# SwiGLU gate/up in seven-product block sums: a fourth such K pair per column block, and two pairs' low parts made by ACT and an adding DMA

## Chip, core and metric

One NeuronCore of a Trainium2 chip runs the whole program; the metric is device time in microseconds. TensorE (PE) multiplies, VectorE (DVE) and ScalarE (ACT) work on vectors, GpSimd (POOL) does little, SyncE (SP) issues the weight loads.

## What is computed

A two-layer encoder trunk on a 256 x 2048 input in float32. Layer 0 mixes by differential attention and a gated MLP, layer 1 by a gated linear recurrence; each layer ends with a SwiGLU FFN of hidden width 5632, and the FFN's first half is what the change touches.

```python
def swiglu(h, w_gate, w_up, w_down):
    return (jax.nn.silu(h @ w_gate) * (h @ w_up)) @ w_down

for l in range(DEPTH):
    h = h + mixer_l(rms_norm(h, mix_norm[l]))
    hn = rms_norm(h, ffn_norm[l])
    h = h + swiglu(hn, ffn_w_gate[l], ffn_w_up[l], ffn_w_down[l])
return rms_norm(h, final_norm)
```

## The kernel before

Weights come from HBM as float32 and are multiplied in three products each: the weight is split into a high part `whi` (ACT rounds the loaded tile `raw` to float32r) and a low part `wlo` (DVE subtracts, raw - whi), the activations likewise into `xh` and `xl`, and PE adds xh*whi, xh*wlo and xl*whi into one bank. `product` (L295 to L300) issues these three matmuls of 128 x 512; L297 and L299 read the high part of the weights, L298 the low part.

**FFN blocks.** The FFN (L394) walks 11 blocks of 512 hidden columns per layer, in the groups 0-1, 2-4, 5-7, 8-10; after each group the down projection of that group runs (`stream`, L128). Block j multiplies all of K = 2048 in eight pairs of 128-row chunks; `gate_up` (L289) handles them one after the other. For pair p one load of 1 MB brings four tiles of 128 x 512: gate and up columns of both chunks. `raw` and `whi` have three buffers, `wlo` two, shared with `stream`. Everything of the split runs ahead of its use by the priority `AHEAD`, and the scheduler writes out one fixed order per engine; each engine works through its order without overtaking.

**Two kinds of pairs.** Write a pair's K chunks and token halves as 2 x 2 blocks. An N pair takes eight products (24 matmuls) into the banks P2, P4, P5, P3. An S pair takes seven products (21 matmuls) into seven banks, with sums of weight tiles in place of some of the tiles: DVE forms four sums (L316 to L318), ACT rounds them to `thi` (L319), DVE makes `tlo` (L322). `thi`, `tlo` and the sums' tile `t` have one buffer each. The sums of activations (`make_combos`, L366) are formed once per layer during block 0, which uses eight N pairs. The string `PAIRS` gives the pattern of the other ten blocks: three S, five N.

**End of a block.** After the last S pair the banks P1, P6 and P7 are combined into `u` (L430 to L432); after the last pair DVE and ACT add up the other banks, apply silu and write `hh` (L444 to L448, L406, L407, L410), which PE transposes (L206) for the down projection.

Of the kernel before, what the change touches and what calls it, by code (L numbers as in the profile page):

```python
# [11 lines left out]
F32 = mybir.dt.float32  # L12
F32R = mybir.dt.float32r
# [3 lines left out]
ALU = mybir.AluOpType  # L17
# [28 lines left out]
WLO_BUFS = 2  # L46
# [26 lines left out]
def trunk(ctx: ExitStack, tc: tile.TileContext, ins, out):  # L73
    nc = tc.nc
# [20 lines left out]
    def bank(tag, shape, name):  # L95
        return psum[tag].tile(shape, F32, tag=tag, name=name)
# [18 lines left out]
    def tick():  # L115
        while pieces:
            try:
                next(pieces[0])
                return
            except StopIteration:  # L120
                pieces.pop(0)
# [162 lines left out]


    P1, P2, P3, P4, P5, P6, P7 = range(7)
    PAIRS = "NSNSNSNN"

    def gate_up(l, j, xs, combos, fx, name, plain, after):  # L289
        pattern = "N" * 8 if plain else PAIRS  # L290
        bk = [bank("mm", [P, NB], f"{name}_ps{i}") for i in range(4 if plain else 7)]
        uses = {"S": [P1, P2, P3, P6, P7, P4, P5], "N": [0, 1, 2, 3] if plain else [P2, P4, P5, P3]}
        seen, final = set(), {b: p for p in range(8) for b in uses[pattern[p]]}

        def product(b, p, x, w, end):  # L295
            (xh, xl), (hi, lo) = x, w
            nc.tensor.matmul(bk[b], xh, hi, start=b not in seen, stop=False)  # L297
            nc.tensor.matmul(bk[b], xh, lo, start=False, stop=False)  # L298
            nc.tensor.matmul(bk[b], xl, hi, start=False, stop=end and final[b] == p)  # L299
            seen.add(b)  # L300

        for p in range(8):
            raw = wpool.tile([P, 4, NB], F32, tag="raw", name=f"{name}_raw{p}")
            whi = wpool.tile([P, 4, NB], F32R, tag="whi", name=f"{name}_whi{p}")
            wlo = wpool.tile([P, 4, NB], F32R, tag="wlo", name=f"{name}_wlo{p}", bufs=WLO_BUFS)
            nc.sync.dma_start(raw, ins["w_gu"][l][j, p])
            fast = pattern[p] == "S"
            with tc.high_priority(offset=AHEAD):
                d = slice(0, 3 if fast else 4)
                nc.scalar.copy(whi[:, d], raw[:, d])  # L310
                if fast:

                    t = fx.tile([P, 4, NB], F32, tag="t", name=f"{name}_t{p}")
                    thi = fx.tile([P, 4, NB], F32R, tag="thi", name=f"{name}_thi{p}")
                    tlo = fx.tile([P, 4, NB], F32R, tag="tlo", name=f"{name}_tlo{p}")
                    nc.vector.tensor_tensor(t[:, 0:2], raw[:, 0:3:2], raw[:, 3:4].broadcast_to([P, 2, NB]), op=ALU.add)  # L316
                    nc.vector.tensor_tensor(t[:, 2], t[:, 0], raw[:, 2], op=ALU.add)
                    nc.vector.tensor_tensor(t[:, 3], t[:, 2], raw[:, 1], op=ALU.add)  # L318
                    nc.scalar.copy(thi, t)  # L319
                nc.vector.tensor_tensor(wlo[:, d], raw[:, d], whi[:, d].bitcast(F32), op=ALU.subtract)  # L320
                if fast:
                    nc.vector.tensor_tensor(tlo, t, thi.bitcast(F32), op=ALU.subtract)  # L322
            xs.get(min(p + 1, 7))
            xh, xl = xs.get(p)
            k0 = p % 2 * 2

            def x(c, b):
                s = slice(b * P, (b + 1) * P)
                return xh[:, k0 + c, s], xl[:, k0 + c, s]

            def w(i):
                return whi[:, i], wlo[:, i]

            if plain:
                for b, c, i in ((0, 0, 0), (0, 1, 1), (1, 0, 0), (1, 1, 1), (2, 0, 3), (2, 1, 2), (3, 0, 3), (3, 1, 2)):
                    product(b, p, x(c, b % 2), w(i), c == 1)
                    if (b, c) == (1, 1):
                        tick()
            elif fast:
                def sums(i):  # L340
                    return combos[p][0][:, i], combos[p][1][:, i]

                def tw(i):
                    return thi[:, i], tlo[:, i]

                product(P1, p, x(0, 0), w(0), True)
                product(P2, p, x(1, 0), w(1), True)
                product(P3, p, sums(2), w(2), True)
                product(P6, p, sums(1), tw(2), True)
                product(P7, p, sums(3), tw(1), True)  # L350
                product(P4, p, x(1, 1), tw(3), True)
                product(P5, p, sums(0), tw(0), True)
            else:
                for c in range(2):
                    product(P2, p, x(c, 0), w(c), c == 1)
                for c in range(2):
                    product(P4, p, x(c, 1), w(c), c == 1)
                for c in range(2):
                    product(P5, p, x(c, 1), w(3 - c), c == 1)
                for c in range(2):  # L360
                    product(P3, p, (combos[p][0][:, c], combos[p][1][:, c]), w(3 - c), c == 1)
            after(p, bk)
            tick()
        return bk

    def make_combos(xs, cp, combos, name):  # L366

        for p in range(8):
            xh, xl = xs.get(p)
            xt = _ap(xh, 0, [[KG * S, 2], [S, KG], [1, S]]).bitcast(F32)  # L370
            k0 = p % 2 * 2
            n = 4 if PAIRS[p] == "S" else 2
            c = [cp.tile([P, n, P], F32R, tag=f"c{p}{i}", name=f"{name}_c{p}{i}", bufs=1) for i in range(2)]
            parts = tmp.tile([P, 2, n, P], F32, tag="hh", name=f"{name}_cp{p}", bufs=2)

            def x(k, b):
                return xt[:, :, k0 + k, b * P:(b + 1) * P]

            if n == 4:

                nc.vector.tensor_tensor(parts[:, :, 0], x(0, 1), x(1, 1), op=ALU.subtract)
                nc.vector.tensor_tensor(parts[:, :, 1], parts[:, :, 0], x(0, 0), op=ALU.subtract)
                nc.vector.tensor_tensor(parts[:, :, 2], parts[:, :, 1], x(1, 0), op=ALU.add)
                nc.vector.tensor_tensor(parts[:, :, 3], x(0, 0), x(0, 1), op=ALU.subtract)
            else:
                for k in range(2):
                    nc.vector.tensor_tensor(parts[:, :, k], x(k, 0), x(k, 1), op=ALU.subtract)
            nc.vector.tensor_tensor(parts[:, 0], parts[:, 0], parts[:, 1], op=ALU.add)
            nc.scalar.copy(c[0], parts[:, 0])
            nc.vector.tensor_tensor(c[1], parts[:, 0], c[0].bitcast(F32), op=ALU.subtract)  # L390
            combos.append(c)
            yield

    def ffn(l, xs, rstd, following):  # L394

        with tc.tile_pool(name=f"hT{l}", bufs=3, reuse_waits="tile") as hp:
            scope = ExitStack()
            fx = scope.enter_context(tc.tile_pool(name=f"fx{l}", bufs=1, reuse_waits="tile"))
# [13 lines left out]
            for blocks in (range(0, 2), range(2, 5), range(5, 8), range(8, 11)):  # L412
                halves = Lazy()
                for j in blocks:
                    n = f"f{l}_{j}"
                    plain = j == 0
# [7 lines left out]
                    def after(p, bk):  # L424
                        if p in (1, 3) and halves.makers:
                            halves.get(len(halves.makers) - (2 if p == 1 else 1))
                        if not plain and p == PAIRS.rindex("S"):
                            with tc.high_priority(offset=2 * AHEAD):
# [4 lines left out]
                                early["u"] = u1, u2, u3  # L433

                    bk = gate_up(l, j, xs, combos, fx, n, plain, after)
                    hh = tmp.tile([P, 2, NB], F32, tag="hh", name=f"{n}_hh", bufs=2)
                    with tc.high_priority(offset=2 * AHEAD):
                        if plain:
                            for b in range(2):
# [33 lines left out]
                name = f"f{l}d{blocks[0]}_"  # L473
# [165 lines left out]
    for b in range(2):  # L639
# [8 lines left out]
        for half in range(2):  # L648
            v = vb[half][:, b, :]
            f = slice(half * NB, (half + 1) * NB)  # L650
# [58 lines left out]
    op = odd.enter_context(tc.tile_pool(name="odd", bufs=2, reuse_waits="tile"))  # L709

    def proj_c(nb, name, **kw):
        return stream(ins["hgrn_w_in"], [nb], ALLK, Groups(xs), f"c_{name}", **kw)[0]
# [103 lines left out]
    for hg in range(4):  # L816
# [30 lines left out]
        for d in range(2):  # L847
            ps = proj_c(4 + 4 * d + hg, f"f{d}{hg}")
            t = op.tile([P, 2, NB], F32, tag=f"f{d}", name=f"f{d}_{hg}", bufs=1)
# [15 lines left out]

    for nb in range(4):
        ps = proj_c(16 + nb, f"g{nb}", after=at_end(early) if nb == 3 else None)
        gt = tmp.tile([P, 2, NB], F32, tag="hh", name=f"g{nb}t", bufs=2)
        gated(ps, gt, True)
        if nb == 3:  # L870
            finish_pieces()
        nc.vector.tensor_tensor(o[nb], gt, o[nb], op=ALU.mult)
        xo.makers.append(lambda nb=nb: to_T(o[nb], xpool, "xT", f"co{nb}", gain_cols(SM_GN, nb)))
# [138 lines left out]
```

## Time and profile before

| | |
|---|---|
| median of 3 runs (lowest, highest) | 2433.96 us (2432.55, 2434.47) |
| the profiled execution | 2432.7 us, of which span 2430.9 us |
| PE, share of the span | 99% (11212 matmuls recorded) |
| DVE / ACT / POOL | 72% / 47% / 3% |
| granted PE clock, mean | 0.998 of full speed |
| loads | 442 MB on SP's queue, 52.1% of the 16 DMA engines |

An engine's busy share is over the whole span; a matmul's own duration (0.39 us here) overlaps that of the next, so PE's rate is read from start to start. In the names of the order rows below `f0_6_whi3` is layer 0, block 6, pair 3; `ps0` to `ps6` are the banks P1 to P7, and `x0_c20` is a sum of activations.

### The profile page before, as it was taken

What the parts mean: (1) busy time and instruction counts of PE and PEld (TensorE: products, weight loads), DVE (VectorE), ACT (ScalarE), POOL (GpSimd) and SP (SyncE); (2) the same over time, 40 slices, a digit from 0 to 9 for tenths busy, and PEclk for the clock granted to TensorE, in tenths of its full rate; (3) what the DMA queues carried; (4) which work ended last, traced back from release to release, by engine and by line L of the source; (5) the groups of instructions that cost most, each with busy time, mean ns of one, the idle gap of its engine ahead of it and who ended that gap; (6) DMA issues with size and microseconds to landing.
All of it is one profiled execution on the core that took longest, in us unless ns stands there. A gap on an engine that the chain in (4) does not pass through costs nothing.

```text
span 2430.9 us, 27555 instructions
## 1 busy us (share of the span) xinstructions
PE 2403.7 (99%) x11212; PEld 1993.8 (82%) x11212; DVE 1747.8 (72%) x1680; ACT 1136.2 (47%) x1048; POOL 72.9 (3%) x72
## 2 busy tenths in 40 slices
PE   8999999999999999999999999999999999999998
PEld 7887878888888888888888888888788888888887
DVE  5658667688678678754758595855777867876884
ACT  5445454445345445454444444444444544544553
POOL 0003000000000000000000000000000000000002
PEclk9999999999999999999999999999999999999999
DMA  7444455555555555555444444445455555565553
GB/s 275 169 160 168 160 180 184 190 194 204 191 202 196 191 198 190 201 198 191 156 145 151 156 139 156 144 168 190 169 195 200 187 201 191 190 208 190 208 208 139
DMA packets 63135, 445.50 MB, mean 183 GB/s; under 512 B 6944, under 2 KB 7200, under 8 KB 9760
## 3 DMA queue, kind: packets, MB, share of 16 engines
q1 hardware_dynamic: 62576, 442.13, 52.1%
q8 instruction: 88, 1.44, 0.2%
q10 hardware_dynamic: 432, 1.60, 0.2%
q14 instruction: 39, 0.32, 0.0%
HBM read 441.61 MB, written 2.10 MB: 183 GB/s over the span
## 4 chain that ended last, share of the span: by engine, by line
PE 94%; DVE 3%; POOL 1%; issue 1%; DMA 1%; ACT 0%; SPq 0%; ACTq 0%; POOLq 0%; DVEq 0%
PE f_ps L298 12%; PE f_ps L297 12%; PE f_ps L299 12%; PE f0d_ps L164 3%; PE f0d_ps L166 3%; PE f0d_ps L165 3%; PE f1d_ps L164 3%; PE f1d_ps L165 3%; PE f1d_ps L166 3%; PE c_f_ps L166 2%; PE c_f_ps L164 2%; PE c_f_ps L165 2%; PE s_l L759 2%; PE c_q_ps L166 1%; PE c_q_ps L164 1%; PE c_q_ps L165 1%
## 5 line engine op out<-in xcount | busy, mean ns | idle before, releaser
L310 ACT CAST f_whi<-f_raw 128x2048 fp32r<-128x2048 f32 (+1 forms) x176 | 311.2, 1768 | 248.7 <-PE f_ps L299 162.5
L320 DVE TENSOR_TENSOR f_wlo<-f_raw,f_whi 128x2048 fp32r<-128x2048 f32 (+1 forms) x176 | 368.7, 2106 | 47.0 <-PE f_ps L298 33.2
L297 PE MATMUL f_ps<-f_whi,f_x 128*128 128x512 f32 x848 | 331.3, 393 | 6.1 <-DVE h L883 3.1
L299 PE MATMUL f_ps<-f_whi,f_x 128*128 128x512 f32 x848 | 330.3, 390 | 0.0
L298 PE MATMUL f_ps<-f_wlo,f_x 128*128 128x512 f32 x848 | 330.1, 389 | 0.0
L297 PEld LDWEIGHTS f_ps<-f_whi,f_x 128*128 128x128 f32 x848 | 159.2, 188 | 38.8 <-ACT f_j L182 6.9
L299 PEld LDWEIGHTS f_ps<-f_whi,f_x 128*128 128x128 f32 x848 | 159.2, 188 | 33.6
L298 PEld LDWEIGHTS f_ps<-f_wlo,f_x 128*128 128x128 f32 x848 | 159.3, 188 | 32.2
L322 DVE TENSOR_TENSOR f_tlo<-f_t,f_thi 128x2048 fp32r<-128x2048 f32 x60 | 137.3, 2288 | 62.7 <-ACT f_thi L319 62.7
L319 ACT CAST f_thi<-f_t 128x2048 fp32r<-128x2048 f32 x60 | 114.8, 1913 | 132.3 <-DVE f_t L318 120.0
L149 ACT CAST f1d__whi<-f1d__raw 128x2048 fp32r<-128x2048 f32 x44 | 84.4, 1919 | 128.4 <-PE f1d_ps L166 97.6
L150 DVE TENSOR_TENSOR f1d__wlo<-f1d__raw,f1d__whi 128x2048 fp32r<-128x2048 f32 x44 | 100.8, 2290 | 60.6 <-PE f1d_ps L165 33.0
L150 DVE TENSOR_TENSOR f0d__wlo<-f0d__raw,f0d__whi 128x2048 fp32r<-128x2048 f32 x44 | 100.7, 2289 | 59.0 <-PE f0d_ps L165 29.3
L149 ACT CAST f0d__whi<-f0d__raw 128x2048 fp32r<-128x2048 f32 x44 | 84.4, 1918 | 122.1 <-PE f0d_ps L166 91.3
L150 DVE TENSOR_TENSOR c_f_wlo<-c_f_raw,c_f_whi 128x2048 fp32r<-128x2048 f32 x32 | 73.3, 2292 | 72.5 <-PE c_f_ps L165 60.5
L164 PE MATMUL c_f_ps<-c_f_whi,c_x 128*128 128x512 f32 x256 | 102.5, 400 | 0.0
L299 PE MATMUL f_ps<-f_whi,x_c 128*128 128x512 f32 x260 | 101.1, 389 | 0.0
L298 PE MATMUL f_ps<-f_wlo,x_c 128*128 128x512 f32 x260 | 101.1, 389 | 0.0
L297 PE MATMUL f_ps<-f_whi,x_c 128*128 128x512 f32 x260 | 101.1, 389 | 0.0
L166 PE MATMUL c_f_ps<-c_f_whi,c_x 128*128 128x512 f32 x256 | 100.2, 392 | 0.0
L165 PE MATMUL c_f_ps<-c_f_wlo,c_x 128*128 128x512 f32 x256 | 99.6, 389 | 0.0
L149 ACT CAST c_f_whi<-c_f_raw 128x2048 fp32r<-128x2048 f32 x32 | 61.2, 1913 | 77.6 <-PE c_f_ps L166 57.6
(536 smaller groups left out, 5637.1 us busy)
## 6 DMA issues: line engine op xcount, KB each, us to landing
f_raw<-in_w_gu SPq DMA_DIRECT2D x176, 1024.0 KB, 4.9
f0d__raw<-in_w_down SPq DMA_DIRECT2D x44, 1024.0 KB, 4.9
f1d__raw<-in_w_down SPq DMA_DIRECT2D x44, 1024.0 KB, 4.9
c_f_raw<-in_hgrn_w_in SPq DMA_DIRECT2D x32, 1024.0 KB, 4.9
eout_raw<-in_even_w_out SPq DMA_DIRECT2D x16, 1024.0 KB, 4.8
c_i_raw<-in_hgrn_w_in SPq DMA_DIRECT2D x16, 1024.0 KB, 4.8
c_q_raw<-in_hgrn_w_in SPq DMA_DIRECT2D x16, 1024.0 KB, 4.8
c_g_raw<-in_hgrn_w_in SPq DMA_DIRECT2D x16, 1024.0 KB, 4.9
```

Of the source, the lines that this page charges most:

```text
L149: nc.scalar.copy(whi[:, d], raw[:, d])
L150: nc.vector.tensor_tensor(wlo[:, d], raw[:, d], whi[:, d].bitcast(F32), op=ALU.subtract)
L164: nc.tensor.matmul(ps[b], xh[:, k, sl], hi[:, k, :], start=first, stop=False)
L165: nc.tensor.matmul(ps[b], xh[:, k, sl], lo[:, k, :], start=False, stop=False)
L166: nc.tensor.matmul(ps[b], xl[:, k, sl], hi[:, k, :], start=False, stop=end)
L297: nc.tensor.matmul(bk[b], xh, hi, start=b not in seen, stop=False)
L298: nc.tensor.matmul(bk[b], xh, lo, start=False, stop=False)
L299: nc.tensor.matmul(bk[b], xl, hi, start=False, stop=end and final[b] == p)
L310: nc.scalar.copy(whi[:, d], raw[:, d])
L319: nc.scalar.copy(thi, t)
L320: nc.vector.tensor_tensor(wlo[:, d], raw[:, d], whi[:, d].bitcast(F32), op=ALU.subtract)
L322: nc.vector.tensor_tensor(tlo, t, thi.bitcast(F32), op=ALU.subtract)
```

## The change

`PAIRS` becomes "SNSNSNSN": four S and four N pairs in the ten blocks that are not plain. An S pair's sums are written over `raw` itself (`t` is gone), after `wlo` has been made from it, so that `raw` is read until `tlo` is made. In all 11 blocks of a layer the low part of the N pairs 3 and 7 (`SUMMED`) is made in another way: ACT writes -whi into a tile `slo` (one buffer), and a DMA issued by POOL loads the same 1 MB of weights again and adds it to that tile. `hh` and the tiles that share its tag get one buffer instead of two. The order of three products in an S pair changes.

```diff
@@ -284,12 +284,14 @@
 
 
     P1, P2, P3, P4, P5, P6, P7 = range(7)
-    PAIRS = "NSNSNSNN"
+    PAIRS = "SNSNSNSN"
+
+    SUMMED = (3, 7)
 
     def gate_up(l, j, xs, combos, fx, name, plain, after):
         pattern = "N" * 8 if plain else PAIRS
         bk = [bank("mm", [P, NB], f"{name}_ps{i}") for i in range(4 if plain else 7)]
-        uses = {"S": [P1, P2, P3, P6, P7, P4, P5], "N": [0, 1, 2, 3] if plain else [P2, P4, P5, P3]}
+        uses = {"S": [P1, P2, P6, P7, P3, P4, P5], "N": [0, 1, 2, 3] if plain else [P2, P4, P5, P3]}
         seen, final = set(), {b: p for p in range(8) for b in uses[pattern[p]]}
 
         def product(b, p, x, w, end):
@@ -302,24 +304,30 @@
         for p in range(8):
             raw = wpool.tile([P, 4, NB], F32, tag="raw", name=f"{name}_raw{p}")
             whi = wpool.tile([P, 4, NB], F32R, tag="whi", name=f"{name}_whi{p}")
-            wlo = wpool.tile([P, 4, NB], F32R, tag="wlo", name=f"{name}_wlo{p}", bufs=WLO_BUFS)
+            if p in SUMMED:
+                wlo = fx.tile([P, 4, NB], F32R, tag="slo", name=f"{name}_slo{p}")
+            else:
+                wlo = wpool.tile([P, 4, NB], F32R, tag="wlo", name=f"{name}_wlo{p}", bufs=WLO_BUFS)
             nc.sync.dma_start(raw, ins["w_gu"][l][j, p])
             fast = pattern[p] == "S"
             with tc.high_priority(offset=AHEAD):
                 d = slice(0, 3 if fast else 4)
                 nc.scalar.copy(whi[:, d], raw[:, d])
                 if fast:
-
-                    t = fx.tile([P, 4, NB], F32, tag="t", name=f"{name}_t{p}")
+                    nc.vector.tensor_tensor(wlo[:, d], raw[:, d], whi[:, d].bitcast(F32), op=ALU.subtract)
+
                     thi = fx.tile([P, 4, NB], F32R, tag="thi", name=f"{name}_thi{p}")
                     tlo = fx.tile([P, 4, NB], F32R, tag="tlo", name=f"{name}_tlo{p}")
-                    nc.vector.tensor_tensor(t[:, 0:2], raw[:, 0:3:2], raw[:, 3:4].broadcast_to([P, 2, NB]), op=ALU.add)
-                    nc.vector.tensor_tensor(t[:, 2], t[:, 0], raw[:, 2], op=ALU.add)
-                    nc.vector.tensor_tensor(t[:, 3], t[:, 2], raw[:, 1], op=ALU.add)
-                    nc.scalar.copy(thi, t)
-                nc.vector.tensor_tensor(wlo[:, d], raw[:, d], whi[:, d].bitcast(F32), op=ALU.subtract)
-                if fast:
-                    nc.vector.tensor_tensor(tlo, t, thi.bitcast(F32), op=ALU.subtract)
+                    nc.vector.tensor_tensor(raw[:, 0:4:3], raw[:, 0:3:2], raw[:, 3:4].broadcast_to([P, 2, NB]), op=ALU.add)
+                    nc.vector.tensor_tensor(raw[:, 2], raw[:, 0], raw[:, 2], op=ALU.add)
+                    nc.vector.tensor_tensor(raw[:, 1], raw[:, 2], raw[:, 1], op=ALU.add)
+                    nc.scalar.copy(thi, raw)
+                    nc.vector.tensor_tensor(tlo, raw, thi.bitcast(F32), op=ALU.subtract)
+                elif p in SUMMED:
+                    nc.scalar.mul(wlo, whi.bitcast(F32), -1.0)
+                    nc.gpsimd.dma_start(wlo, ins["w_gu"][l][j, p], accum_op=ALU.add)
+                else:
+                    nc.vector.tensor_tensor(wlo, raw, whi.bitcast(F32), op=ALU.subtract)
             xs.get(min(p + 1, 7))
             xh, xl = xs.get(p)
             k0 = p % 2 * 2
@@ -345,10 +353,10 @@
 
                 product(P1, p, x(0, 0), w(0), True)
                 product(P2, p, x(1, 0), w(1), True)
+                product(P6, p, sums(1), tw(2), True)
+                product(P7, p, sums(3), tw(3), True)
                 product(P3, p, sums(2), w(2), True)
-                product(P6, p, sums(1), tw(2), True)
-                product(P7, p, sums(3), tw(1), True)
-                product(P4, p, x(1, 1), tw(3), True)
+                product(P4, p, x(1, 1), tw(1), True)
                 product(P5, p, sums(0), tw(0), True)
             else:
                 for c in range(2):
@@ -371,7 +379,7 @@
             k0 = p % 2 * 2
             n = 4 if PAIRS[p] == "S" else 2
             c = [cp.tile([P, n, P], F32R, tag=f"c{p}{i}", name=f"{name}_c{p}{i}", bufs=1) for i in range(2)]
-            parts = tmp.tile([P, 2, n, P], F32, tag="hh", name=f"{name}_cp{p}", bufs=2)
+            parts = tmp.tile([P, 2, n, P], F32, tag="hh", name=f"{name}_cp{p}", bufs=1)
 
             def x(k, b):
                 return xt[:, :, k0 + k, b * P:(b + 1) * P]
@@ -433,7 +441,7 @@
                                 early["u"] = u1, u2, u3
 
                     bk = gate_up(l, j, xs, combos, fx, n, plain, after)
-                    hh = tmp.tile([P, 2, NB], F32, tag="hh", name=f"{n}_hh", bufs=2)
+                    hh = tmp.tile([P, 2, NB], F32, tag="hh", name=f"{n}_hh", bufs=1)
                     with tc.high_priority(offset=2 * AHEAD):
                         if plain:
                             for b in range(2):
...
```

The same change of `bufs` stands once more in the gating of layer 1.

**What moves.** ACT's order around block 6 of layer 0, before, from the high part of pair 2 to that of pair 6:

```order
L310 CAST f0_6_whi2_5352<-f0_6_raw2_5351 128x2048
L406 ACTIVATE f0_5_s1_5264<-f0_5_g1_4986,f0_rstd_3003 128x512
L310 CAST f0_6_whi3_5382<-f0_6_raw3_5381 128x1536
L209 CAST f0_5T_x_5343<-f0_5T_tp0_5344 128x512
L310 CAST f0_6_whi4_5424<-f0_6_raw4_5423 128x2048
L319 CAST f0_6_thi3_5387<-f0_6_t3_5386 128x2048
L310 CAST f0_6_whi5_5454<-f0_6_raw5_5453 128x1536
L310 CAST f0_6_whi6_5495<-f0_6_raw6_5494 128x2048
```

and now, from the rounded sums of pair 0 to the negation of pair 7:

```order
L324 CAST f0_6_thi0_5303<-f0_6_raw0_5297 128x2048
L315 CAST f0_6_whi3_5404<-f0_6_raw3_5403 128x2048
L327 ACTIVATE f0_6_slo3_5405<-f0_6_whi3_5404 128x2048
L324 CAST f0_6_thi2_5375<-f0_6_raw2_5369 128x2048
L315 CAST f0_6_whi4_5442<-f0_6_raw4_5441 128x1536
L315 CAST f0_6_whi5_5476<-f0_6_raw5_5475 128x2048
L209 CAST f0_5T_x_5361<-f0_5T_tp1_5434 128x512
L315 CAST f0_6_whi6_5506<-f0_6_raw6_5505 128x1536
L324 CAST f0_6_thi4_5447<-f0_6_raw4_5441 128x2048
L315 CAST f0_6_whi7_5546<-f0_6_raw7_5545 128x2048
L327 ACTIVATE f0_6_slo7_5547<-f0_6_whi7_5546 128x2048
```

The negations (L327) stand right behind the high parts of pairs 3 and 7, and the rounded sums of pair 2 stand behind the first of them. (L209 rounds a transposed tile, as before.) DVE's order where block 5 ends and block 6 begins, before:

```order
L320 TENSOR_TENSOR f0_6_wlo0_5280<-f0_6_raw0_5278,f0_6_whi0_5279 128x2048
L444 TENSOR_TENSOR f0_5_g0_4985<-f0_5_ps1_4988,f0_5_u0_5189 128x512
L322 TENSOR_TENSOR f0_6_tlo1_5315<-f0_6_t1_5313,f0_6_thi1_5314 128x2048
L445 TENSOR_TENSOR f0_5_g1_4986<-f0_5_ps3_4990,f0_5_u2_5191 128x512
L446 TENSOR_TENSOR f0_5_hh_5255<-f0_5_ps4_4991,f0_5_u1_5190 128x512
L447 TENSOR_TENSOR f0_5_hh_5255<-f0_5_ps4_4991,f0_5_u2_5191 128x512
L448 TENSOR_TENSOR f0_5_hh_5255<-f0_5_ps2_4989,f0_5_hh_5255 128x512
L407 SCALAR_TENSOR_TENSOR f0_5_g0_4985<-f0_5_g0_4985,f0_rstd_3003,f0_5_s0_5261 128x512
L407 SCALAR_TENSOR_TENSOR f0_5_g1_4986<-f0_5_g1_4986,f0_rstd_3003,f0_5_s1_5264 128x512
L410 SCALAR_TENSOR_TENSOR f0_5_hh_5255<-f0_5_hh_5255,f0_rstd_3003,f0_5_g0_4985 128x512
L410 SCALAR_TENSOR_TENSOR f0_5_hh_5255<-f0_5_hh_5255,f0_rstd_3003,f0_5_g1_4986 128x512
L320 TENSOR_TENSOR f0_6_wlo1_5310<-f0_6_raw1_5308,f0_6_whi1_5309 128x1536
```

and now:

```order
L452 TENSOR_TENSOR f0_5_g0_5001<-f0_5_ps1_5004,f0_5_u0_5237 128x512
L322 TENSOR_TENSOR f0_6_raw0_5297<-f0_6_raw0_5297 128x512
L453 TENSOR_TENSOR f0_5_g1_5002<-f0_5_ps3_5006,f0_5_u2_5239 128x512
L415 SCALAR_TENSOR_TENSOR f0_5_g0_5001<-f0_5_g0_5001,f0_rstd_3006,f0_5_s0_5280 128x512
L454 TENSOR_TENSOR f0_5_hh_5274<-f0_5_ps4_5007,f0_5_u1_5238 128x512
L455 TENSOR_TENSOR f0_5_hh_5274<-f0_5_ps4_5007,f0_5_u2_5239 128x512
L456 TENSOR_TENSOR f0_5_hh_5274<-f0_5_ps2_5005,f0_5_hh_5274 128x512
L415 SCALAR_TENSOR_TENSOR f0_5_g1_5002<-f0_5_g1_5002,f0_rstd_3006,f0_5_s1_5283 128x512
L418 SCALAR_TENSOR_TENSOR f0_5_hh_5274<-f0_5_hh_5274,f0_rstd_3006,f0_5_g0_5001 128x512
L418 SCALAR_TENSOR_TENSOR f0_5_hh_5274<-f0_5_hh_5274,f0_rstd_3006,f0_5_g1_5002 128x512
L323 TENSOR_TENSOR f0_6_raw0_5297<-f0_6_raw0_5297 128x512
L330 TENSOR_TENSOR f0_6_wlo1_5333<-f0_6_raw1_5331,f0_6_whi1_5332 128x2048
```

Before, the sums of block 6's first S pair (pair 1, on `t`) stand ahead of these rows, and the low part of pair 1 comes right behind the ending. The sums of block 6's first pair now straddle the ending of block 5, and the low part of pair 1 is the second instruction behind it. PE's order at the same place, now:

```order
L301 MATMUL f0_5_ps2_5005<-f0_5_whi7_5244,x0_c71_3009 128x512
L299 MATMUL f0_6_ps0_5290<-f0_6_whi0_5298,f00_x_2612 128x512
L300 MATMUL f0_6_ps0_5290<-f0_6_wlo0_5299,f00_x_2612 128x512
L301 MATMUL f0_6_ps0_5290<-f0_6_whi0_5298,f00_x_2612 128x512
L299 MATMUL f0_6_ps1_5291<-f0_6_whi0_5298,f00_x_2612 128x512
L300 MATMUL f0_6_ps1_5291<-f0_6_wlo0_5299,f00_x_2612 128x512
L301 MATMUL f0_6_ps1_5291<-f0_6_whi0_5298,f00_x_2612 128x512
L299 MATMUL f0_6_ps1_5291<-f0_6_whi1_5332,f00_x_2612 128x512
L299 MATMUL f0_6_ps0_5290<-f0_6_whi2_5370,f01_x_2665 128x512
L206 MATMUL f0_5T_tp0_5362<-ident_89,f0_5_hh_5274 128x128 x4
L300 MATMUL f0_6_ps1_5291<-f0_6_wlo1_5333,f00_x_2612 128x512
```

Eight matmuls and four transposes stand between block 5's last product and the first that reads `wlo1`; before, 24 matmuls of pair 0 stood there ahead of pair 1. PE's first read of `slo3` is the 64th row from that read of `wlo1` on, its first read of `slo7` is 88 rows further, and `whi3` is read for the last time 22 rows after the first read of `slo3`. In the changed program's allocation raw1, raw3, raw5 and raw7 of a block share one of the three buffers of `raw`, raw0 and raw4 another, raw2 and raw6 the third: raw3's load waits until `wlo1` is made, raw4's until `tlo0` is.

## Rows read from the trace of the kernel before

**Rows 1.** The page: span, busy time, and the chain that ended last, by engine.
```profile
span 2430.9 us, 27555 instructions
...
PE 2403.7 (99%) x11212; PEld 1993.8 (82%) x11212; DVE 1747.8 (72%) x1680; ACT 1136.2 (47%) x1048; POOL 72.9 (3%) x72
...
PE 94%; DVE 3%; POOL 1%; issue 1%; DMA 1%; ACT 0%; SPq 0%; ACTq 0%; POOLq 0%; DVEq 0%
```

**Rows 2.** Engines by stretch, 546 to 549 us and most of layer 0's FFN.
```profile
core 0: us, PE busy (x) PEld busy (x) DVE busy (x) ACT busy (x) POOL busy (x), PEclk, DMA share, GB/s
546.00:549.00 3.00, 3.00 (x17) 2.51 (x16) 3.00 (x4) 2.25 (x2) 0.00 (x0) 1.00 0.98 382
645.00:1000.00 355.00, 355.00 (x1583) 292.87 (x1582) 276.27 (x222) 168.11 (x111) 0.00 (x0) 1.00 0.56 196
```

**Rows 3.** Who waited for whom: total us, times, longest us.
```profile
PE e_tp L206 <- DMA h<-in_x: 6.1, 1, 6.1
PE f_ps L297 <- DVE h L883: 3.1, 1, 3.1
...
ACT f_whi L310 <- PE f_ps L299: 162.5, 74, 6.0
ACT f_thi L319 <- DVE f_t L318: 120.0, 43, 6.2
```

**Rows 4.** The tile tlo: what PE's idle time before it ended with (us, times).
```profile
  DVE f_tlo L322: 4.9, 15
```

**Rows 5.** PE in order of time, 602.1 to 603.75 us: start, duration; eight matmuls.
```profile
602.14 0.39 PE L298 MATMUL f_ps<-f_wlo,f_x 128*128 128x512 f32 x1
...
603.73 0.39 PE L299 MATMUL f_ps<-f_whi,f_x 128*128 128x512 f32 x1
```

**Rows 6.** DVE's groups of instructions by form: busy us, mean ns.
```profile
L320 DVE TENSOR_TENSOR f_wlo<-f_raw,f_whi 128x2048 fp32r<-128x2048 f32 x116 | 264.8, 2289 | 47.0 <-PE f_ps L298 33.2 <-issue 11.2 <-PE f1d_ps L165 1.1
L322 DVE TENSOR_TENSOR f_tlo<-f_t,f_thi 128x2048 fp32r<-128x2048 f32 x60 | 137.3, 2288 | 62.7 <-ACT f_thi L319 62.7
L320 DVE TENSOR_TENSOR f_wlo<-f_raw,f_whi 128x1536 fp32r<-128x1536 f32 x60 | 105.1, 1752 | 0.0
...
L316 DVE TENSOR_TENSOR f_t<-f_raw 128x1024 f32<-128x1024 f32 x60 | 73.3, 1222 | 20.4 <-DMA f_raw<-in_w_gu 19.6 <-DVE f_wlo L320 0.3
...
L318 DVE TENSOR_TENSOR f_t<-f_t,f_raw 128x512 f32<-128x512 f32 x60 | 41.3, 689 | 1.1
```

**Rows 7.** ACT in order of time, 547 to 553 us: high parts and rounded sums.
```profile
547.33 1.91 ACT L310 CAST f_whi<-f_raw 128x2048 fp32r<-128x2048 f32 x1
549.16 1.91 ACT L319 CAST f_thi<-f_t 128x2048 fp32r<-128x2048 f32 x1
552.18 1.49 ACT L310 CAST f_whi<-f_raw 128x1536 fp32r<-128x1536 f32 x1 [1.11 <-PE f_ps L299]
```

**Rows 8.** DVE in order of time where block 2 ends and block 3 begins.
```profile
536.60 0.68 DVE L447 TENSOR_TENSOR f_hh<-f_ps,f_u 128x512 f32<-128x512 f32 x1
537.20 0.68 DVE L448 TENSOR_TENSOR f_hh<-f_ps,f_hh 128x512 f32<-128x512 f32 x1
537.80 1.53 DVE L407 SCALAR_TENSOR_TENSOR f_g<-f_g,f_rstd,f_s 128x512 f32<-128x512 f32 x2
539.25 1.41 DVE L410 SCALAR_TENSOR_TENSOR f_hh<-f_hh,f_rstd,f_g 128x512 f32<-128x512 f32 x2
540.57 1.75 DVE L320 TENSOR_TENSOR f_wlo<-f_raw,f_whi 128x1536 fp32r<-128x1536 f32 x1
```

**Rows 9.** The chain that ended last, at 546 us: four transposes.
```profile
546.17 0.44 PE f_2T_tp L206 x4
```

**Rows 10.** SP's queue: what its loads waited for: total us, times, longest us.
```profile
SPq L306 <- DVE f_wlo L320: 653.5, 128, 9.3
```

**Rows 11.** DMA issues: KB each, median us from issue to landing.
```profile
f_raw<-in_w_gu SPq DMA_DIRECT2D x176, 1024.0 KB, 4.9
```

**Rows 12.** PE in order of time at the start of the program, 7.7 to 10.1 us.
```profile
7.77 0.80 PE L164 MATMUL e_q_ps<-e_q_whi,e_x 128*128 128x512 f32 x1
8.89 0.80 PE L165 MATMUL e_q_ps<-e_q_wlo,e_x 128*128 128x512 f32 x1 [0.33 <-DVE e_q_wlo L150]
...
10.07 0.40 PE L165 MATMUL e_q_ps<-e_q_wlo,e_x 128*128 128x512 f32 x1
```

More of the change, by code (lines that the diff above doesn't have):

```diff
@@ L867, in trunk @@
         ps = proj_c(16 + nb, f"g{nb}", after=at_end(early) if nb == 3 else None)
-        gt = tmp.tile([P, 2, NB], F32, tag="hh", name=f"g{nb}t", bufs=2)
+        gt = tmp.tile([P, 2, NB], F32, tag="hh", name=f"g{nb}t", bufs=1)
         gated(ps, gt, True)
```

## Prediction

> **What bounds the kernel now.** I read the page first. The span is 2430.9 us, PE is busy for 2403.7 of it, and the chain that ended last runs over PE for 94% [rows 1]. The windows show the same inside layer 0's FFN: PE is busy for all of 355 us at granted clock 1.00, while DVE has 276.27 of them, ACT 168.11 and the loads a DMA share of 0.56 [rows 2]. So time is lost or won only where PE idles or issues fewer rows. The list of waits tells how near the other engines are: PE's largest waits are single ones of 6.1 and 3.1 us at the start and the end, whereas ACT waits 162.5 us for PE to free `whi` and 120.0 us for DVE's sums [rows 3]. The preparation is thus ahead of PE, but through few buffers. The one place of an S pair where PE idles is `tlo`: 15 waits, 4.9 us in all over 60 S pairs [rows 4]. The profiled execution took 2432.7 us, 1.3 less than the median of the runs; the sum is made against it and 1.3 is added at the end.
>
> **A. Fewer products.** Each of the 20 blocks that are not plain turns one N pair into an S pair, 24 matmuls into 21. In PE's order of time eight matmuls start within 1.59 us, seven steps, 0.227 us each [rows 5]. 60 x 0.227 = **-13.6 us**. For this DVE is hardly relieved. With the durations by form [rows 6], an N pair's low part costs 2.29 and an S pair 1.75 + 1.22 + 2 x 0.69 + 2.29 = 6.64: per block 5 x 2.29 + 3 x 6.64 = 31.4 before, 2 x 2.29 + 4 x 6.64 = 31.1 now. ACT gets 44 negations at 1.91 (nearest row: its cast of the same tile) and 20 more rounded sums at 1.91 [rows 7]; PE hides the durations themselves, since ACT has half its time free [rows 2], and what counts is their place, in C and D. The single buffer of `hh` costs nothing: its next writer comes a whole block later, and the sums of activations lie beside block 0's products; uncovered, one hand-over of 0.1 us a block. The order of three products in an S pair moves no work.
>
> **B. The boundary of two blocks.** The last product of a block releases DVE's ending. In the trace of before the last of the `hh` sums, the gating and the start of the next low part follow one another: 0.60 us for L448, 1.45 for two L407, 1.32 for two L410 [rows 8]. Now DVE has, from the last product to the end of `wlo1`, 0.60 + 0.72 (one L415) + 1.32 + 0.69 (the sum L323) + 2.29 = 5.62 us [rows 6, 8]. PE has eight matmuls, 1.82, and four transposes, 0.44 [rows 9], together 2.26, and then reads `wlo1`. Before, 24 matmuls (5.4) and the transposes covered the same ending. So PE idles 5.62 - 2.26 = 3.36 us where a block follows a block directly: blocks 3, 4, 6, 7, 9 and 10 of both layers, 12 times, **+40 us**. With starts (5.4) or full durations and a hand-over (5.9) it is 38 to 44.
>
> **C. S pairs that are fed later.** Sums now stand in `raw`, which is held until `tlo` is made; SP's loads already spend 653.5 us waiting for DVE to be done with a buffer [rows 10], so these loads start later. The rounded sums of pair 2 also stand behind a negation of 1.91 us on ACT. Low end: the 80 pairs wait as the 60 did, 4.9 x 20 / 60 = +2 [rows 4]. High end: the whole negation shows at `thi` in 20 blocks, +38. I take 0.33 us, the mean of the present waits, for three pairs of four, 60 x 0.33 = **+20 us**.
>
> **D. The adding load.** This is the largest term, and no row shows such a transfer. Let L be the time from the end of the negation to the landing of the sum. POOL is otherwise idle in the FFN and nothing but these loads stands in its order there, so its own wait for the negation delays nobody else.
> - Pair 3: raw3's load starts when `wlo1` is made. The load takes 4.9 [rows 11], the high part and the negation 1.91 each [rows 7], three hand-overs 0.3: 9.0. In that time PE goes from its first read of `wlo1` to `slo3`, 61 matmuls and some transposes: 61 x 0.227 + 0.44 + 0.4 of waits = 14.7. The slack is 5.7; PE stalls L - 5.7.
> - Pair 7: after `slo3` has landed PE reads it in 22 rows, 5.0; then ACT rounds `whi6` (1.49, held by the buffer of `whi3`), the sums of pair 4 (1.83 start to start), `whi7` (1.83) and negates (1.91) [rows 7], with hand-overs 12.4. PE has 88 rows, 20.0. The slack is 7.6; PE stalls L - 7.6.
>
> Together 2L - 13.3 in each of 22 blocks. Low end for L: the plain load of 1 MB, 4.9, which would stall nothing. High end: two such loads in series behind one raw load at the full rate of 382 GB/s [rows 2], 2 x 4.9 + 2.75 = 12.6. The transfer reads its destination, adds and writes, so the nearest row is the load, twice: **L = 10**. Then 6.7 x 22 = **+147 us**; with the ends 0 and +262 (11.9 x 22).
>
> The trace has no adding transfer to hold a rule against. The Trainium skill ("Collectives: The Full Stack", section "Why ReduceScatter is half of AllGather") says that an add in the DMA engine is dear not by the adding but by a second source read; by it and the row of 382 GB/s an estimate of L is 4.9 + 2.75 = 7.65, and the sum would come to +91 instead of +194. No run here shows it yet.
>
> **Sum.** -13.6 + 40 + 20 + 147 = +194; 2432.7 + 194 + 1.3 = **2628 us**. A difference under 0.2% (4.9 us) can't be told from none here.
>
> **The rivals.**
> 1. *The adding load costs one more pass of its bytes and no more*: L = 7.65 by the rate row [rows 2]. Stalls 1.95 + 0.05 a block, +44; total +91, **2525 us**. For it: the loads' engines are 44% free. Against it: SP's next loads run at the same time.
> 2. *The adding load is hidden*, L up to 5.7, because it is no dearer than a plain load. Then A + B + C remain: +47, **2481 us**. Against it: two reads and a write can hardly go as fast as one of each.
> 3. *The adding load is slow*, for example by many small pieces or by competing with raw loads: at L = 20 the stalls are 26.7 x 22 = 587, **3069 us**. It decides from L = 13 on.
> 4. *PE's clock falls in the gaps.* Gaps of about 4 us come some 40 times. In the trace the first two matmuls behind 6 us without work took 0.80 us and later ones 0.40 [rows 12], though the granted clock of that stretch reads 1.00; if all 22 products between a gap and the last read of `whi3` ran at half speed, 5 us each, it would be 40 x 5 = +200, **2828 us**. The Trainium skill ("TensorE: Matmul & The Clock Gate", Part 1) has the clock at 1.2 GHz after PE has been idle; before, the granted clock shows nothing of it, because PE hardly idles.
> 5. *Faster: PE stays the bound.* The mechanism is the three matmuls saved per block, with all preparation arriving in time; the place is each of the 20 blocks, the price -13.6, and it decides from stalls under 0.68 us a block. It needs L below 5.7 and a boundary where DVE gets through its ending in 2.3 us. For it: before, no ending shows as a wait of PE at all [rows 3]. Against it: 5.62 us of DVE's rows. **2420 us**. If the stalls just eat the saving, the time is the same.
>
> **How the numbers follow.** Chances: the forecast (L from 9 to 13) 0.40; rival 1 (L from 6 to 9) 0.20; rival 2 0.08; rival 3 0.17; rival 4 0.08; faster 0.05; the same 0.02. All but the last two are slower: 0.93. The range goes from just under rival 2 (2475) to rival 4 (2830, which also is L = 14.7); outside lie faster, same and most of rival 3, just under 0.2.
>
> **What would show it.** In the changed profile: matmuls fewer by 60; PE's waits on `slo` as the largest of all, some 4 us for pair 3 and 2 for pair 7, with L in the DMA list near 10; waits at `wlo1` of 3.4 us, 12 times, whose chain goes over DVE's L418 and L323; small waits at `thi` and `tlo`. B is wrong if PE waits at `wlo1` less than 2 us; D is wrong if the list shows a landing under 6 or over 13 us, or if `raw` loads slow beside it; the clock rival shows as a granted clock below 1.00 in the FFN.

## The result, and the profile after

The changed kernel takes 2660.99 us (median of 4 runs, 2655.96 to 2670.75), before 2434.22 us: ratio 1.0931, 95% interval 1.0906 to 1.0957, or 227 us slower. The prediction said 2628 us with a range of 2475 to 2830. The total is close; its make-up is not, as the profile shows. In the views below, PE is TensorE, PEld its weight loads, and a landing is the end of a transfer.

The page of the changed kernel: span, busy times, the sixteen DMA engines by queue (packets, MB, share of the span) and the chain by engine, against [rows 1].

```profile
span 2658.4 us, 27661 instructions
...
PE 2485.9 (94%) x11152; PEld 2025.5 (76%) x11152; DVE 1751.2 (66%) x1720; ACT 1245.8 (47%) x1112; POOL 110.6 (4%) x116
...
q1 hardware_dynamic: 62576, 442.13, 46.6%
q0 software_dynamic: 6336, 46.14, 8.8%
...
PE 69%; DMA 17%; ACT 6%; DVE 5%; issue 2%; POOL 1%; SPq 0%; ACTq 0%; POOLq 0%
```

PE issues 60 matmuls fewer and is yet busy 82.2 us longer, and it idles 2658.4 - 2485.9 = 172.5 us where it idled 27.2. Both matter. Transfers, 1% of the chain before, are 17% of it now. The idle part stands in the list of PE's waits (total us, times, longest us), against [rows 3]:

```profile
PE f_ps L300 <- DMA f_slo<-in_w_gu: 106.7, 36, 5.7
PE f_ps L300 <- DVE f_wlo L330: 27.1, 12, 2.3
PE e_tp L206 <- DMA h<-in_x: 6.0, 1, 6.0
PE f_ps L299 <- DVE h L891: 3.5, 1, 3.5
PE f_ps L299 <- DVE h L279: 3.3, 1, 3.3
PE f_ps L300 <- DVE f_tlo L325: 3.1, 8, 0.5
```

The adding loads and the twelve block boundaries make 134 us of it. Smaller waits show at the weight loads of the FFN's products, where before, apart from the start of each FFN, only `tlo` stood, first those of before:

```profile
PEld f_ps L298 <- DVE f_tlo L322: 4.8, 14, 0.6
```

and now:

```profile
PEld f_ps L299 <- ACT f_thi L324: 9.9, 19, 1.3
PEld f_ps L299 <- ACT f_whi L315: 8.6, 18, 0.6
PEld f_ps L300 <- DVE f_tlo L325: 7.8, 17, 0.8
```

That is 26.3 - 4.8 = 21.5 us more. What makes PE's busy time longer is seen behind one wait, in PE's order of time at 659 to 670 us:

```profile
659.68 0.39 PE L299 MATMUL f_ps<-f_whi,f_x 128*128 128x512 f32 x1
664.83 0.79 PE L300 MATMUL f_ps<-f_slo,f_x 128*128 128x512 f32 x1 [4.76 <-DMA f_slo<-in_w_gu]
665.42 0.63 PE L301 MATMUL f_ps<-f_whi,f_x 128*128 128x512 f32 x1
665.85 0.63 PE L299 MATMUL f_ps<-f_whi,f_x 128*128 128x512 f32 x1
...
670.07 0.40 PE L300 MATMUL f_ps<-f_slo,f_x 128*128 128x512 f32 x1
670.30 0.39 PE L301 MATMUL f_ps<-f_whi,f_x 128*128 128x512 f32 x1
```

and in the windows there (columns as in [rows 2]):

```profile
665.00:670.00 5.00, 5.00 (x12) 3.94 (x13) 1.12 (x3) 0.72 (x1) 0.00 (x0) 0.50 0.96 406
670.00:680.00 10.00, 10.00 (x47) 8.24 (x47) 7.50 (x9) 4.29 (x3) 0.00 (x0) 1.00 0.00 1
```

After 4.76 us of waiting the granted clock is 0.50, the 1.2 GHz level, and matmuls start 0.43 us apart, not 0.227: twelve in 5 us where 22 would fit. The wait thus costs 4.76 us and then some 2.5 more. The mean granted clock of the whole run fell from 0.998 to 0.968: 0.032 x 2658.4 - 0.002 x 2430.9 = 80 us of clock that PE did not get, some of it while waiting. Counted in starts, the matmuls within twenty rows behind the 48 waits on `slo` and at `wlo1` lost 63 us.

The account of the 227.5 us of span: idle +145.3 (the two large waits 134, the rest the boundary's transposes and small waits), busy +82.2. The latter is -13.6 for the matmuls saved, 60 to 80 for the clock and some 20 for the weight loads.

The adding loads' time from issue to landing (44 of them, min, median, max), and two pieces of the chain in block 9 of layer 0, first that of pair 3, then that of pair 7:

```profile
DMA to landing us min/median/max: 7.7/8.5/12.7
```

```profile
1026.11 8.24 DMA f_slo<-in_w_gu
...
1047.10 12.40 DMA f_slo<-in_w_gu
```

The median hides two cases. Over the 22 blocks pair 3's load lands after 8.3 us in the median and PE waits about 45 us for it in all; pair 7's lands after 11.8 us and PE waits 62 us. Around the second piece (the DMA view from 1040 to 1064 us) three raw loads for the next block share the engines:

```profile
q1 hardware_dynamic: 432, 3.15, 36.7%
q0 software_dynamic: 144, 1.05, 21.5%
...
f_raw<-in_w_gu SPq DMA_DIRECT2D x3, 1024.0 KB, 8.5
```

In 24 us the raw loads took 0.367 x 24 / 3 = 2.9 us each of all sixteen engines, the adding one 5.2, together 14.0. The raw loads begin to be issued at 1044.9 us and `slo7` lands at 1059.5, so the engines had work nearly all that time. Two of the raw loads land before the load that PE waits for, the third 1.3 us behind it. They are slowed as well: 8.5 us in the median, against 5.0 over the whole run.

### The profile page after: what moved, and what is told of

It reads as the page before. It is cut to its first block, busy times and chain, and to the rows that moved or that the text cites. A ratio compares the mean times of both kernels' runs of the same rounds, so it can differ in the third digit from the quotient of the medians.

```text
span 2658.4 us, 27661 instructions
## 1 busy us (share of the span) xinstructions
PE 2485.9 (94%) x11152; PEld 2025.5 (76%) x11152; DVE 1751.2 (66%) x1720; ACT 1245.8 (47%) x1112; POOL 110.6 (4%) x116
## 4 chain that ended last, share of the span: by engine, by line
PE 69%; DMA 17%; ACT 6%; DVE 5%; issue 2%; POOL 1%; SPq 0%; ACTq 0%; POOLq 0%
DMA f_slo<-in_w_gu 14%; PE f_ps L300 6%; PE f_ps L301 6%; PE f_ps L299 5%; PE f0d_ps L164 3%; PE f0d_ps L165 3%; PE f0d_ps L166 3%; PE f1d_ps L166 3%; PE f1d_ps L164 3%; PE f1d_ps L165 3%; DMA f_raw<-in_w_gu 3%; ACT f_whi L315 2%; ACT f_slo L327 2%; PE c_f_ps L166 2%; PE c_f_ps L164 2%; PE c_f_ps L165 2%
## 5 line engine op out<-in xcount | busy, mean ns | idle before, releaser
L299 PE MATMUL f_ps<-f_whi,f_x 128*128 128x512 f32 x768 | 321.3, 419 | 7.9 <-DVE h L891 3.5
L301 PE MATMUL f_ps<-f_whi,f_x 128*128 128x512 f32 x768 | 317.9, 417 | 0.0
L325 DVE TENSOR_TENSOR f_tlo<-f_raw,f_thi 128x2048 fp32r<-128x2048 f32 x80 | 183.3, 2291 | 129.2 <-ACT f_thi L324 129.2
L300 PE MATMUL f_ps<-f_slo,f_x 128*128 128x512 f32 x272 | 128.0, 471 | 106.8 <-DMA f_slo<-in_w_gu 106.7
L300 PE MATMUL f_ps<-f_wlo,f_x 128*128 128x512 f32 x496 | 199.6, 402 | 27.1 <-DVE f_wlo L330 27.1
L317 DVE TENSOR_TENSOR f_wlo<-f_raw,f_whi 128x1536 fp32r<-128x1536 f32 x80 | 140.5, 1756 | 103.6 <-PE f_ps L300 69.9
L324 ACT CAST f_thi<-f_raw 128x2048 fp32r<-128x2048 f32 x80 | 152.2, 1903 | 72.7 <-DVE f_raw L323 72.5
L300 PEld LDWEIGHTS f_ps<-f_slo,f_x 128*128 128x128 f32 x272 | 60.8, 224 | 137.3 <-DMA f_slo<-in_w_gu 124.4
L330 DVE TENSOR_TENSOR f_wlo<-f_raw,f_whi 128x2048 fp32r<-128x2048 f32 x52 | 119.0, 2288 | 23.3 <-ACT f_whi L315 20.1
L300 PEld LDWEIGHTS f_ps<-f_wlo,f_x 128*128 128x128 f32 x496 | 95.9, 193 | 49.5 <-DVE f_wlo L330 29.9
L300 PE MATMUL f_ps<-f_tlo,x_c 128*128 128x512 f32 x240 | 95.8, 399 | 3.3 <-DVE f_tlo L325 3.1
```

The source lines that it names most:

```text
L324: nc.scalar.copy(thi, raw)
L325: nc.vector.tensor_tensor(tlo, raw, thi.bitcast(F32), op=ALU.subtract)
```

## Experiments

All differences below are against the kernel before, run on the same chip.

**The S pairs without the adding loads.** The low parts of pairs 3 and 7 are DVE's again, in the two buffers of `wlo`.

```diff
-    SUMMED = (3, 7)
+    SUMMED = ()
```

> The changed kernel with the low parts of pairs 3 and 7 made by DVE again; the four S pairs and their sums over raw stay. Theory (the adding loads and the half clock behind their waits are most of the loss): the 107 us of waits on slo go, and nearly all matmuls at half rate with them; what is left is the boundary, 12 waits of 2.3 us and some 10 us of half clock behind them, less 13.6 for the saved matmuls: 2450 to 2480 us. Rival A (the four S pairs with sums over raw are the loss, because raw is held and loads start late): PE's waits move to wlo and tlo and the time stays over 2540 us.

Measured: 2528.5 us, ratio 1.0373 (1.0356 to 1.0391), +92 us, granted clock 0.980. The waits on `slo` are gone and 134 us with them, so the adding loads are the larger half. But the time lies 48 us above the theory's range for the rest, and 11 us under Rival A's; of the waits that Rival A named, `tlo` has only 18.4 us, at the weight loads. PE's waits (the transposes have six lines like the second, 23.1 us in all):

```profile
PE f_ps L300 <- DVE f_wlo L330: 26.2, 12, 2.3
...
PE f_2T_tp L206 <- DVE f_hh L418: 3.9, 4, 1.7
```

The boundary costs 49 us of waits here and puts the clock down: 146 matmuls of half rate, 0.2 us each, stand behind the twelve waits at `wlo1`, 29 us.

**The adding loads without the fourth S pair.** The pattern of before, pairs 2 and 6 by adding load.

```diff
-    PAIRS = "SNSNSNSN"
-
-    SUMMED = (3, 7)
+    PAIRS = "NSNSNSNN"
+
+    SUMMED = (2, 6)
```

> The other half of the change alone: three S pairs in the order of before (first pair an N pair), sums over raw, and the low parts of the N pairs 2 and 6 by negation and adding load. Theory: the boundary waits at wlo go, the waits on slo stay at 2 to 4.5 us each and put the clock to half speed behind them as in the changed kernel: granted clock about 0.97, 2530 to 2640 us. Rival A (the S pairs are the loss): under 2470 us, with few waits on slo.

Measured: 2576.83 us, ratio 1.0566 (1.0547 to 1.0586), +141 us, clock 0.979; 38 waits on `slo`, 85.7 us, the longest 4.3. No boundary wait of more than 0.2 us is left, as 24 matmuls of an N pair stand first again. This is as the theory had it.

**Sums over raw alone.** `PAIRS` as before, `SUMMED` empty; the sums' place, the single `hh` buffer and the order of three products in an S pair stay of the change.

> Before's three S pairs and all low parts on DVE, with only the sums written over raw and hh in one buffer. Theory: raw is held longer, but PE has enough lead: no wait over 1 us in the FFN, 2434 to 2446 us, granted clock 1.00. Rival A (holding raw is dear): the loads land late in each S pair, over 0.5 us in 60 pairs, above 2465 us.

Measured: 2454.90 us, ratio 1.0076 (1.0061 to 1.0091), +19 us. Neither number was right: the longest wait of PE inside the blocks is 2.05 us, the clock is at 0.996, but there are 50 small waits at the weight loads for `tlo` (15.7 us, before 4.8) and 12 for `whi` (9.1). That `raw` is held is seen in two more lists. ACT's waits for a raw load before it can round it, before and here, and the loads on SP's queue that wait here until `tlo` is made:

```profile
ACT f_whi L310 <- DMA f_raw<-in_w_gu: 12.3, 11, 1.9
```

```profile
ACT f_whi L315 <- DMA f_raw<-in_w_gu: 153.7, 58, 5.3
...
SPq L311 <- DVE f_tlo L325: 175.6, 52, 7.0
```

So writing the sums over `raw` has a price of its own. How much of the 19 us is due to it, and how much to the `hh` buffer and the order of products, this run does not separate.

**No adding.** The load into `slo` replaces the negated high part, it does not add to it.

```diff
-                    nc.gpsimd.dma_start(wlo, ins["w_gu"][l][j, p], accum_op=ALU.add)
+                    nc.gpsimd.dma_start(wlo, ins["w_gu"][l][j, p])
```

> The changed kernel with the load into slo not adding (the low parts of pairs 3 and 7 are then the weights themselves); the negation, its place and POOL's issue stay. Theory (the time to landing is engine work shared with the raw loads; the adding makes 5.2 us of work on the sixteen engines out of 2.9): landing falls from 8.2 to about 6 us for pair 3 and from 12.4 to about 10 for pair 7, waits on slo from 107 to 30 to 50 us, half-rate matmuls to about half: 2520 to 2570 us. Rival B (the adding is the whole delay): landing near 5 in both, waits under 15 us, 2460 to 2490 us. Rival C (POOL's issue and the queue behind raw loads are the delay, not the adding): landing and time hardly change, over 2630 us.

Measured: 2518.70 us, ratio 1.0329 (1.0310 to 1.0347), +83 us, 144 less than with the adding; clock 0.992 in the profiled execution, which took 2509.6 us. The page has the same bytes on the same queue (MB, share of the engines) and the landing; the list of waits has PE's:

```profile
q0 software_dynamic: 6336, 46.14, 4.7%
...
f_slo<-in_w_gu POOLq DMA_DIRECT2D x44, 1024.0 KB, 6.9
```

```profile
PE f_ps L300 <- DMA f_slo<-in_w_gu: 10.2, 8, 2.9
```

A load takes 0.047 x 2507.3 / 44 = 2.7 us of all engines without adding and 0.088 x 2658.4 / 44 = 5.3 with it. The landing falls from 8.3 to 5.5 us for pair 3 and from 11.8 to 7.7 for pair 7 (medians of 22), the waits from 106.7 to 10.2 us. The theory's time is missed by 1 us only, but its waits of 30 to 50 us did not come. Rival B is right about the waits; its landing near 5 holds for pair 3 alone, and its time is 29 us too low, as the twelve waits at `wlo1` (27.1 us) are still there. Rival C falls. The waits fell much more than the landing because a wait is only what exceeds PE's slack.

The Trainium skill ("Collectives: The Full Stack", section "Why ReduceScatter is half of AllGather") says that an add in the DMA engine costs a second source read, not the addition; the factor of 5.3 to 2.7 agrees with it.

**A third low-part buffer.** All low parts by DVE, those of pairs 3 and 7 still in `slo`.

```diff
-    SUMMED = (3, 7)
+    SUMMED = ()
+    THIRD = (3, 7)
...
-            if p in SUMMED:
+            if p in THIRD:
                 wlo = fx.tile([P, 4, NB], F32R, tag="slo", name=f"{name}_slo{p}")
```

> Four S pairs with sums over raw, the low parts of pairs 3 and 7 still written into the tile slo, but by DVE's subtraction; no negation, no second load. slo is then only a third buffer for low parts. Theory (the boundary waits of e1 come from the two buffers of wlo: the low part of pair 1 must wait for the last product of pair 7, which reads the other buffer's tile, and so falls behind the ending): the waits at wlo1 go, no wait of PE over 1.7 us in the blocks, granted clock 0.99 or more, 2435 to 2460 us. Rival (DVE has too much to do with four S pairs, whatever the buffers): waits at wlo, tlo or hh of 40 us and more stay, over 2495 us.

Measured: 2448.28 us, ratio 1.0062 (1.0047 to 1.0077), +15 us, clock 0.996, as the theory had it. PE's largest waits:

```profile
PE f_ps L301 <- DVE f_tlo L326: 8.7, 6, 1.5
PE e_tp L206 <- DMA h<-in_x: 6.2, 2, 5.5
```

DVE does all the work of the first experiment (1834.9 us busy, there 1838.2), the boundary waits are gone, and the loss is 77 us smaller. DVE's order now has `wlo1` ahead of the block's ending. In the first experiment that was barred, as `wlo1` takes the buffer that the last products of pair 7 read; in the changed kernel it was not barred (pair 7 has `slo`), only placed so by the scheduler. So the boundary is a matter of that order, and DVE's load is not the bound. A rest of small waits stays: 22.8 us for `tlo` and 8.8 for `thi` at the weight loads.

**One adding load per block.** As the third buffer, with `SUMMED` holding only pair 3, then only pair 7.

> As e5, but pair 3 by negation and adding load as in the change; pair 7 by DVE into slo. Theory: 22 adding loads landing in 8 to 9 us; the boundary waits, which delay raw3's chain as well, go, and PE comes to slo3 sooner by them, so its waits grow to 2.5 to 5 us each, with half-rate matmuls behind them: e5 plus 22 times 5, 2540 to 2590 us. Rival (only pair 7's loads, which share the engines with three raw loads, are dear): within 25 us of e5.

> As e5, but pair 7 by negation and adding load; pair 3 by DVE into slo. Theory: landing 10 to 12.5 us beside the raw loads of the next block's pairs, 22 waits of 3 to 5 us, each with some 2 us of half rate behind it: e5 plus 100 to 140 us, 2550 to 2600 us. Rival (with one adding load a block its chain has room, as the summed slack of 7.6 us in the prediction says): waits under 1 us, within 25 us of e5.

Measured: pair 3 alone 2603.83 us, ratio 1.0702 (1.0686 to 1.0717), +171; pair 7 alone 2602.53 us, ratio 1.0698 (1.0682 to 1.0714), +169. Both theories' ranges were passed by 3 to 14 us, both rivals fall far behind. PE's waits on `slo`, with pair 3 alone and with pair 7 alone:

```profile
PE f_ps L301 <- DMA f_slo<-in_w_gu: 92.4, 22, 6.4
```

```profile
PE f_ps L301 <- DMA f_slo<-in_w_gu: 74.1, 22, 6.5
```

and the adding loads in the list of DMA issues (KB, median us to landing), in the same order:

```profile
f_slo<-in_w_gu POOLq DMA_DIRECT2D x22, 1024.0 KB, 11.4
```

```profile
f_slo<-in_w_gu POOLq DMA_DIRECT2D x22, 1024.0 KB, 10.4
```

Each adds some 155 us to the third-buffer kernel, both together 212: half the adding loads cost three quarters of the price. The two come to it in different ways. With pair 3 alone the load itself lands later, after 11.4 us in the median where pair 3 had 8.3 in the changed kernel, while PE comes to it only 0.6 us sooner behind the negation (6.6 us, there 7.2). With pair 7 alone the load lands sooner (10.4 us, there 11.8), but PE comes 1.3 us sooner too (6.9, there 8.2), and half of the boundary is back, the waits at `wlo` and 21 us at the transposes:

```profile
PE f_ps L301 <- DVE f_wlo L331: 13.5, 6, 2.3
```

So this second run is not the price of an adding load alone. Each wait moves the starts of the loads and of PE's next reads, and the stalls are not terms that add.

**Work put into the gap.** The changed kernel with useless matmuls ahead of pair 7.

```diff
+            if p == 7 and not plain:
+                fill = bank("tr", [P, 2, S], f"{name}_fill")
+                for _ in range(14):
+                    nc.tensor.matmul(fill, xh[:, k0, :P], whi[:, 0], start=True, stop=True)
```

> The changed kernel with 14 matmuls of no use (3.2 us, into the free transpose bank) put ahead of pair 7's products in the 20 blocks that are not plain: 280 matmuls more. Theory (behind a wait of 4 us the matmuls run at half rate because PE stood idle): waits on slo7 fall from 4.3 to about 1 us, the matmuls behind them run at 0.227 us, the granted clock rises to 0.98 or more, and the time falls by 20 to 60 us although PE does 64 us more work. Rival (the slow matmuls come from the transfers running beside them, not from PE's idling): the matmuls behind slo7 stay at 0.43 us, the time stays or grows. The fill also shifts the scheduler's order at some block boundaries.

Measured: 2567.41 us, ratio 1.0559 (1.0541 to 1.0576), +134 us: 93 us faster than the changed kernel with 280 matmuls more, where the theory had 20 to 60; clock 0.990. In the 20 blocks that have the fill PE waits for `slo7` once, 0.35 us; the waits that are left, 51 us, are those of pair 3 and of the two plain blocks. PE in order of time, the fill of block 4 and what follows, and the window there:

```profile
648.15 3.34 PE L345 MATMUL f_fill<-f_whi,f_x 128*128 128x512 f32 x14
651.32 0.39 PE L299 MATMUL f_ps<-f_whi,f_x 128*128 128x512 f32 x1
651.55 0.39 PE L300 MATMUL f_ps<-f_slo,f_x 128*128 128x512 f32 x1
651.77 0.39 PE L301 MATMUL f_ps<-f_whi,f_x 128*128 128x512 f32 x1
```

```profile
651.50:657.00 5.50, 5.50 (x26) 4.53 (x26) 3.44 (x6) 1.49 (x3) 0.00 (x0) 1.00 0.97 410
```

The products behind `slo7` start 0.23 us apart at granted clock 1.00 while the DMA share is 0.97. In the changed kernel the same products of the same block, beside a share of 0.96, ran at 0.50. So the half rate comes with PE's standing idle, not with the transfers. The gain of 93 us is not the clock's alone: the fill moved the scheduler's order, and the twelve waits at `wlo1` are gone too. How much each part gave was not separated.

**Weights' own product first.** The third-buffer kernel with P3 ahead of P6 and P7 again.

```diff
+                product(P3, p, sums(2), w(2), True)
                 product(P6, p, sums(1), tw(2), True)
                 product(P7, p, sums(3), tw(3), True)
-                product(P3, p, sums(2), w(2), True)
```

> As e5 (third buffer, all low parts by DVE), and in an S pair the product into P3, which reads the high and low part of the weights alone, stands again ahead of the two that read the sums, as before the change. Theory (what e5 still loses against before are many waits of about 0.45 us for thi and tlo, 31 us in all at the weight loads): three matmuls, 0.68 us, cover most of them; they fall under 12 us and the time lies at 2425 to 2440 us, level with before within 0.3% or a little faster. Rival (the loss lies in raw being held, so that everything of an S pair comes later whatever PE reads first): no change from e5, 2443 to 2452 us.

Measured: 2450.95 us, ratio 1.0062 (1.0050 to 1.0074), no change from the third buffer. The small waits at the weight loads fell only from 31.6 to 26.4 us. The rival's time came out. That `raw` is held is the reading that fits, as ACT waits for raw loads here as in the run with the sums over `raw` alone, but no run takes it away by itself:

```profile
ACT f_whi L316 <- DMA f_raw<-in_w_gu: 159.7, 62, 6.8
```

None of the versions run beats the kernel before.

## Why the prediction was right, and where its steps were not

- **A, fewer products, -13.6:** 60 matmuls fewer, as said. Its time can't be seen by itself.
- **B, the boundary, +40:** twelve waits of 2.26 us at `wlo1`, 27.1, and twelve of 0.27 at the transposes, 3.2: 30. DVE's part was right: at the start of block 9 of layer 0 it takes from 1010.24 to 1015.71, 5.47 us, predicted 5.62. PE's own rows took longer than 2.26: from its first matmul of block 9 at 1010.04 to the wait 3.47, of which the transposes, which themselves wait for `hh`, have 1.1. What the step left out is the half clock behind nine of the twelve waits.

```profile
1010.24 0.69 DVE L456 TENSOR_TENSOR f_hh<-f_ps,f_hh 128x512 f32<-128x512 f32 x1
...
1013.43 2.28 DVE L330 TENSOR_TENSOR f_wlo<-f_raw,f_whi 128x2048 fp32r<-128x2048 f32 x1
```

```profile
1012.97 0.55 PE L206 MATMUL f_8T_tp<-ident,f_hh 128*128 128x128 f32 x3 [0.27 <-DVE f_hh L418]
1015.77 0.80 PE L300 MATMUL f_ps<-f_wlo,f_x 128*128 128x512 f32 x1 [2.26 <-DVE f_wlo L330]
```

- **C, later feeding, +20:** 21.5 us more at the weight loads. The prediction read the 4.9 us of [rows 4] as PE's idling; they were nearly all the weight loads' too. That `raw` is held is seen in the third experiment; how much the negation ahead of pair 2's sums adds was not separated. The size came from the mean of the old waits, and its fit is luck.
- **D, the adding load, +147:** 106.7 us. The slack of pair 7 was right: from `slo3`'s landing to the end of pair 7's negation the chain took 1046.8 - 1034.4 = 12.4 us, as worked out. The slack itself, from the negation's end to PE's read, was 8.2 us for pair 7 in the median, worked out 7.6, and 7.2 for pair 3, worked out 5.7. L was one number of 10 and is two: 8.24 for that block's pair 3, for which I had the larger stall, and 12.40 for its pair 7 beside the next block's raw loads, where PE then waited 4.57 us. In all blocks together pair 3 cost about 45 us, forecast 4.3 x 22 = 95, and pair 7 62, forecast 2.4 x 22 = 53. The prediction's own sign against this step, raw loads that slow beside the adding one, came: 8.5 us instead of 5.0.
- **The clock:** the failed step. Rival 4 stood beside the forecast with a chance of 0.08; it is a part of every case with gaps, not a case of its own. It is worth 60 to 80 us, where the forecast had none. Behind all 17 waits of 3.9 us and more, 6 to 13 matmuls ran at half rate. The prediction says that before the granted clock shows nothing of this, and that is a misreading: behind a wait for POOL, ahead of the FFN, the trace of before has it (columns as in [rows 2]).

```profile
242.19 2.08 PE L661 MATMUL sv<-e_b0t,wsT 128*128 128x256 f32 x4 [2.55 <-POOL e_b0t L653]
```

```profile
241.80:245.20 3.40, 3.01 (x7) 2.47 (x8) 3.37 (x4) 0.97 (x2) 2.01 (x2) 0.51 0.54 227
```

That the forecast's 194 and the 227 measured lie so close is luck: D was 40 us too large, B 10, and the clock, 60 to 80, was missing. The direction rested on sounder ground: the adding experiments confirm that PE waits for the adding load, and rivals 2 and 5 fall. Rival 1 had the right mechanism (one more pass, a factor of two on the engines), but not the sharing of the engines. That sharing stood under rival 3, but at 20 us to landing, where the longest was 12.7.

The Trainium skill ("TensorE: Matmul & The Clock Gate", Part 1) has the clock at 1.2 GHz after idling; the 0.50 of the window at 665 us agrees, and it would have been right to put this into the sum.

## What to carry to other kernels

A kernel that keeps TensorE at 99% has a second price for every new wait of some microseconds: the matmuls behind it can run at half rate, so that here the large waits, 134 us, cost about one and a half times their length. A transfer that adds was two transfers to the DMA engines here (5.3 us of all sixteen, not 2.7); ask what else is queued there when it is issued, and not for its median. And before an engine is relieved, look at whether it or a buffer is the limit: one more low-part buffer took 77 us off the first experiment with DVE's work unchanged.

## What was not expected of the hardware

Waits of 2.26 us could be enough for the half rate: behind nine of the twelve at `wlo1` in the changed kernel 8 to 13 matmuls ran at it, behind three none. Behind the ten waits on `slo` of 1.73 us and less there were at most two. The length of the wait alone does not tell: of the nine waits on `slo` from 1.88 to 2.59 us five brought the half rate and four did not.
